# Moving the 256-column matmul streams of a fused two-block kernel out of two-bank PSUM tiles into single banks

## The chip, the cores and the metric

The kernel runs on one core of one Trainium2 chip. The metric is the device time of one execution in microseconds (us), as the median of three runs. "Faster" or "slower" below means a change of that time.

## The reference, cut to what matters

Two transformer-like blocks run one after the other on 256 tokens of width 1024, all in fp32:

```python
# block 1
proj = rms_norm(x, ln_mix_g) @ w_in
a_out = gmlp_spatial_gating(...)          # 512 channels
b_out = banded_chunk_attention(...)       # 8 heads of 64
x = x + concat([a_out, b_out]) @ w_out
x = x + peer_ffn(rms_norm(x, ln_ffn_g), w_query, sub_keys, expert_u, expert_v)
# block 2
y_pool, y_sb, y_x = (three branches) @ (w_pool_o, w_sb_o, w_x_o)
merged = gates[0] * y_pool + gates[1] * y_sb + gates[2] * y_x
h = x + rmsnorm(merged @ w_out, norm_mix_post)
gu = rmsnorm(h, norm_ffn_pre) @ w_ffn_in
out = h + rmsnorm((silu(gu[:, :2816]) * gu[:, 2816:]) @ w_ffn_out, norm_ffn_post)
```

peer_ffn picks 16 of 16384 experts per head and token; the kernel computes it densely, as two passes over all 128 x 128 experts with gates that are zero for those not picked.

## The kernel before, in words

Every large product is made of three fp32r matmuls per 128 x 128 weight block: high part of the weight times high part of the activation (line 180), the same weight times the low part of the activation (181), and the low part of the weight times the high activation (182). One *projection* is `project`: 8 weight blocks of a [128, 1024] weight tile, 24 matmuls of 256 columns (the 256 tokens), all accumulated in one 256-column stretch of PSUM, which is half a bank.

Weights stream through one pipeline that follows a fixed list. `ahead()` is called once per projection: it issues the DMA of the next raw tile (line 166), the ScalarE copy that makes its high part (`wh`, 171), runs an optional function `between`, and then issues the VectorE subtraction that makes the low part (`wl`, 116). Each engine works strictly in the order in which the program issues its instructions, so whatever stands behind one of these copies on ScalarE or VectorE waits for it.

PSUM has eight banks, given out by one pool with three tags of two buffers each: `u` and `g` are tiles of one bank (`bank()`), `y` is a tile of two banks (`pair()`). A new tile of a tag takes the buffer of the tile before the last one of the same tag, and a matmul into it waits for the last instruction that read that buffer.

The places that the change and the prediction touch, in order of the program:

- `mixer_a`, the q/k projections (loop over i = 0 to 7): their outputs alternate between `u` and `y`. Each is read twice on ScalarE, as a square (line 345) and as a scaled copy (346). For i of 2 and more these two stand behind the weight copies of `ahead()`. For i = 0 and 1 they come first, but behind what the previous step issued, among it four squares of x (line 214).
- `mixer_a`, `out(half, jp)`: eight output tiles of two projections of 12 matmuls each, e = 0 and 1. Seven write the two banks of a `y` tile, and one VectorE add (507) takes both into x. The last (half 0, jp 3) writes two `g` banks, with one add each (517), so that the first add can run beside the second projection.
- `experts`: the first two query projections run interleaved (`project2`, 198 to 201) into the two banks of a `y` tile.
- `mixer_c`, cross branch (loop over i = 0, 1): four projections of six matmuls into one `y` tile of 1024 columns, then one VectorE multiply (1055) of all 1024. Then the loop over j = 0 to 7: two projections of 12 matmuls into a `y` tile, one VectorE multiply (1067), and for j below 6 a gate projection into `u`.
- `ffn`: gate and up projections of 22 feature tiles j. Tile 0 goes to a `y` tile, tile 1 to `u`, tiles from 2 on to `g` and `u` in turn. The row norm `rs` (1181) is ready only after tile 3; the first VectorE multiply (1144) of tile 0 stands behind it.

Of the kernel before, what the change touches and what calls it, by code (L numbers as in the profile page):

```python
# [15 lines left out]
KD = 8  # L16
# [39 lines left out]
class Prog:  # L56
# [136 lines left out]
    def project2(self, pss, ws, xh, xl):  # L193

        for k in range(KD):
            for ps, w in zip(pss, ws):
                wh, wl = self.cols(w, k)
                self.mm(ps, wh, xh[:, k, :], start=(k == 0), stop=False)
                self.mm(ps, wl, xh[:, k, :], start=False, stop=False)
            for ps, w in zip(pss, ws):  # L200
                self.mm(ps, self.cols(w, k)[0], xl[:, k, :], start=False, stop=(k == KD - 1))
# [86 lines left out]
    def mixer_a(self):  # L288
# [3 lines left out]
        with tc.tile_pool(name="sa", bufs=1) as sa, tc.tile_pool(name="we", bufs=2) as we:  # L292
# [35 lines left out]
            for i in range(8):  # L328
                ps = self.pair()[:, 0, 0:S] if i % 2 else bank()
# [150 lines left out]
            def out(half, jp, gates=()):  # L480
                w = self.take()
                last = not half and jp == 3
                if last:
                    ps = [bank("g"), bank("g")]
                else:
                    pair = self.pair()[:, :, 0:S]
                    ps = [pair[:, 0, :], pair[:, 1, :]]

                def part(es, ks):
                    for e in es:  # L490
                        for k in ks:
                            wh, wl = self.cols(w, e * 4 + k)
                            self.mm3(ps[e], wh, wl, cath[:, half * 4 + k, :], catl[:, half * 4 + k, :], k == 0, k == 3)
# [6 lines left out]
                if not last:  # L500
# [5 lines left out]
                    def between():  # L506
                        tt(out=x, in0=pair, in1=x, op=ALU.add)
# [5 lines left out]
                for e in range(2):  # L513
                    j = 2 * jp + e
                    if last:
                        part((e,), range(4))
                        tt(out=self.x[:, j, :], in0=ps[e], in1=self.x[:, j, :], op=ALU.add)
# [163 lines left out]
    def experts(self):  # L681
        nc, tc, a, c = self.nc, self.tc, self.a, self.c
        with tc.tile_pool(name="sg", bufs=1) as sg:
# [32 lines left out]
            for hp in range(16):  # L716
                if hp == 0:
                    first = self.pair()
                    first = [first[:, 0, 0:S], first[:, 1, 0:S]]
# [138 lines left out]
    def mixer_c(self):  # L858
        nc, tc, a, c = self.nc, self.tc, self.a, self.c
        mm, act, tt, ts, stt = self.mm, self.act, self.tt, self.ts, self.stt  # L860
        with tc.tile_pool(name="sc", bufs=1) as sc, tc.tile_pool(name="wc", bufs=1) as wc:
# [187 lines left out]
            for i in range(2):  # L1049
                w = self.take()  # L1050
                ps = self.pair().rearrange("p e (j t) -> p (e j) t", j=2)
                for j in range(4):
                    self.project(ps[:, j, :], w, brh, brl, 8, 2, j * 2)
                g = gate[:, 16 + 4 * i:20 + 4 * i, :]
                self.ahead(between=lambda: tt(out=g, in0=ps, in1=g, op=ALU.mult))
            late = []
            for j in range(KD):
                w = self.take()
                ys = self.pair()
                for b in range(2):  # L1060
                    self.project(ys[:, b, 0:S], w, brh, brl, 4 * b, 4, 4 * b)

                def merge():
# [3 lines left out]
                    tt(out=m, in0=ys[:, :, 0:S], in1=gate[:, j:j + 9:8, :], op=ALU.mult)  # L1067
# [260 lines left out]
```

## Time and profile before

| what | value |
|---|---|
| median of 3 runs | 1305.72 us (1305.24 to 1305.84) |
| the profiled execution | 1305.5 us |
| its span, first to last instruction | 1303.7 us |
| TensorE (PE) busy | 1291.5 us, 99% |
| VectorE (DVE), ScalarE (ACT) busy | 73%, 52% |
| mean granted TensorE clock | 0.999 |

All times of the trace are counted from the start of the span. "Busy" of PE counts overlapping matmuls once; one 256-column matmul is shown as about 0.28 us long, but the next starts some 0.115 us later, so what counts is the distance between starts. "Wait" rows name the engine and line whose signal ended an idle time. The reading goes from the chain of work that ended last, to the waits of PE, to the distance between matmul starts, and then to the places where a PSUM buffer changes hands.

### The profile page before, as it was taken

The numbers are of one execution on the slowest core, as the hardware profiler recorded it, in microseconds if no ns is written. First come the engines' busy times: TensorE is split into PE (matmuls) and PEld (weight loads), VectorE is DVE, ScalarE is ACT, GpSimd is POOL, SyncE is SP. The second block draws the span as 40 slices with busy tenths as digits, with TensorE's granted clock in tenths as the row PEclk, the third lists the DMA queues.
The fourth block names the chain that finished last, engine by engine and source line by source line (L and its number), as shares of the span: only waits on it lengthen the run. The fifth ranks groups of instructions, "written<-read, shape, count | busy, mean of one in ns | idle before, by whom it ended". The sixth has DMA issues, their size and how long they took to land.

```text
span 1303.7 us, 27324 instructions
## 1 busy us (share of the span) xinstructions
PE 1291.5 (99%) x11518; PEld 1256.1 (96%) x11518; DVE 945.8 (73%) x1517; ACT 673.0 (52%) x935; POOL 1.6 (0%) x9
## 2 busy tenths in 40 slices
PE   9999999999999999999999999999999999999998
PEld 8799999999999999999999999999999999999986
DVE  5567899878888887799985665556567576776743
ACT  7575454454544444444444554444677646655542
POOL 0000000000000000000000000000000000000000
PEclk9999999999999999999999999999999999999999
DMA  8545466655655555555556755564644456455652
GB/s 273 188 128 179 162 196 197 196 191 193 190 184 176 170 173 176 182 173 170 175 165 194 257 186 193 192 194 149 228 147 147 147 193 217 160 189 193 194 186 74
DMA packets 65211, 237.14 MB, mean 182 GB/s; under 512 B 7360, under 2 KB 7488, under 8 KB 64576
## 3 DMA queue, kind: packets, MB, share of 16 engines
q1 hardware_dynamic: 64800, 233.30, 54.8%
q10 hardware_dynamic: 288, 2.10, 0.5%
q8 instruction: 90, 1.47, 0.4%
q14 instruction: 33, 0.27, 0.1%
HBM read 233.27 MB, written 2.10 MB: 181 GB/s over the span
## 4 chain that ended last, share of the span: by engine, by line
PE 94%; DVE 3%; ACT 2%; issue 1%; DMA 1%; SPq 0%; DVEq 0%; ACTq 0%
PE u L180 20%; PE u L181 19%; PE u L182 19%; PE g L180 7%; PE g L181 7%; PE g L182 7%; PE y L180 3%; PE y L182 3%; PE y L181 3%; PE y L669 2%; DVE wl L116 1%; ACT wh L171 1%; PE y L870 1%; DMA raw<-w_in_t 1%; PE y L846 1%
## 5 line engine op out<-in xcount | busy, mean ns | idle before, releaser
L116 DVE TENSOR_TENSOR wl<-raw,wh 128x1024 fp32r<-128x1024 f32 x426 | 519.1, 1222 | 271.4 <-ACT wh L171 270.7
L171 ACT ACTIVATE wh<-raw 128x1024 fp32r<-128x1024 f32 x426 | 451.1, 1060 | 485.5 <-PE u L181 376.6
L180 PE MATMUL u<-nh,wh 128*128 128x256 f32 x2176 | 609.6, 280 | 0.2 <-ACT big L1017 0.2
L181 PE MATMUL u<-nl,wh 128*128 128x256 f32 x2176 | 602.4, 277 | 0.9 <-DVE nl L733 0.5
L182 PE MATMUL u<-nh,wl 128*128 128x256 f32 x2176 | 601.7, 277 | 0.7 <-DVE wl L116 0.7
L180 PEld LDWEIGHTS u<-nh,wh 128*128 128x128 f32 x2176 | 408.7, 188 | 2.8 <-issue 1.7
L181 PEld LDWEIGHTS u<-nl,wh 128*128 128x128 f32 x2176 | 408.9, 188 | 2.0 <-DVE nl L272 0.7
L182 PEld LDWEIGHTS u<-nh,wl 128*128 128x128 f32 x2176 | 408.5, 188 | 1.0 <-DVE wl L116 0.9
L180 PE MATMUL g<-nh,wh 128*128 128x256 f32 x680 | 188.2, 277 | 0.0
L182 PE MATMUL g<-nh,wl 128*128 128x256 f32 x680 | 187.8, 276 | 0.0
L181 PE MATMUL g<-nl,wh 128*128 128x256 f32 x680 | 187.8, 276 | 0.0
L180 PEld LDWEIGHTS g<-nh,wh 128*128 128x128 f32 x680 | 127.6, 188 | 0.3 <-issue 0.3
L182 PEld LDWEIGHTS g<-nh,wl 128*128 128x128 f32 x680 | 127.7, 188 | 0.0
L181 PEld LDWEIGHTS g<-nl,wh 128*128 128x128 f32 x680 | 127.7, 188 | 0.0
L658 DVE TENSOR_TENSOR og<-ob,gT 128x1024 f16<-128x1024 f16 x64 | 41.4, 688 | 1.1
L654 DVE TENSOR_TENSOR oa<-iot,i1T 128x2048 f16<-128x2048 f16 x32 | 39.0, 1218 | 0.0
L669 PE MATMUL y<-og,oa 128*128 128x64 f16 x1024 | 35.4, 193 | 0.0
L669 PEld LDWEIGHTS <-oa 128*128 128x128 f16 x1024 | 31.6, 98 | 1.1
L1017 ACT ACTIVATE big<-u 128x256 f32<-128x256 f32 x30 | 11.5, 383 | 27.2 <-PE u L182 27.2
L181 PE MATMUL y<-brl,wh 128*128 128x256 f32 x80 | 22.4, 280 | 0.0
L180 PE MATMUL y<-brh,wh 128*128 128x256 f32 x80 | 22.3, 279 | 0.0
L182 PE MATMUL y<-brh,wl 128*128 128x256 f32 x80 | 22.3, 279 | 0.0
(342 smaller groups left out, 1388.8 us busy)
## 6 DMA issues: line engine op xcount, KB each, us to landing
raw<-peer_u SPq DMA_DIRECT2D x128, 512.0 KB, 3.6
raw<-peer_v SPq DMA_DIRECT2D x128, 512.0 KB, 3.6
raw<-w_in_t SPq DMA_DIRECT2D x50, 512.0 KB, 3.9
raw<-ffn_in SPq DMA_DIRECT2D x44, 512.0 KB, 4.0
raw<-ffn_out SPq DMA_DIRECT2D x22, 512.0 KB, 3.5
raw<-w_out SPq DMA_DIRECT2D x16, 512.0 KB, 3.6
raw<-w_query SPq DMA_DIRECT2D x16, 512.0 KB, 3.5
raw<-w_in_v SPq DMA_DIRECT2D x12, 512.0 KB, 4.4
```

The costliest lines, as they stand in the source:

```text
L116: self.tt(out=lo, in0=raw, in1=h.bitcast(F32), op=ALU.subtract)
L171: self.act(h, raw, AF.Copy)
L180: self.mm(ps, wh, xh, start=start, stop=False, **kw)
L181: self.mm(ps, wh, xl, start=False, stop=False, **kw)
L182: self.mm(ps, wl, xh, start=False, stop=stop, **kw)
L654: tt(out=split(oa), in0=row(0, P), in1=runs(i1T[:, d], P), op=ALU.is_equal)
L658: tt(out=split(og[:, s]), in0=split(ob), in1=runs(gT[:, s, d], 64), op=ALU.mult)
L669: nc.tensor.matmul(ps[:, j, :], oa[:, j, :], og[:, s, j, :], start=(s == 0), stop=(s == 1))
L846: self.mm(ps[:, j, :], w[:, k * P:(k + 1) * P], self.mem[:, k, :], start=(k == 0), stop=(k == KD - 1))
L870: mm(pss[:, t, 0:256], self.mem[:, 4 * i + k, t * P:(t + 1) * P], w[:, k * 256:(k + 1) * 256], start=(4 * i + k == 0), stop=(4 * i + k == ...
L1017: copy = lambda v, scale=1.0: lambda ps: act(v, ps, AF.Copy, scale=scale)
```

## The change

All 256-column fp32r streams that wrote a `y` tile write single banks of `u` or `g` now. The q/k projections all write `u`. In `out` the two halves of a tile share one `u` bank, the last tile too, and its second half is started with a matmul that does not clear the bank where e = 1 of jp = 0 would clear what e = 0 has summed. `project2` takes a list of outputs that share a bank with another. The first two query projections take two `g` tiles. The cross branch takes two `g` tiles per step and two VectorE multiplies of 512 columns in place of one of 1024, the branch loop takes one `g` tile per step, and tile 0 of `ffn` takes a `g` tile. The count of matmuls and their order stay; two VectorE instructions are added.

```diff
-    def project2(self, pss, ws, xh, xl):
+    def project2(self, pss, ws, xh, xl, shared=()):
+        kw = dict(skip_group_check=len(shared) > 0)
         for k in range(KD):
+            for i, (ps, w) in enumerate(zip(pss, ws)):
+                wh, wl = self.cols(w, k)
+                self.mm(ps, wh, xh[:, k, :], start=(k == 0 and i not in shared), stop=False, **kw)
+                self.mm(ps, wl, xh[:, k, :], start=False, stop=False, **kw)
             for ps, w in zip(pss, ws):
-                wh, wl = self.cols(w, k)
-                self.mm(ps, wh, xh[:, k, :], start=(k == 0), stop=False)
-                self.mm(ps, wl, xh[:, k, :], start=False, stop=False)
-            for ps, w in zip(pss, ws):
-                self.mm(ps, self.cols(w, k)[0], xl[:, k, :], start=False, stop=(k == KD - 1))
+                self.mm(ps, self.cols(w, k)[0], xl[:, k, :], start=False, stop=(k == KD - 1), **kw)
...
             for i in range(8):
-                ps = self.pair()[:, 0, 0:S] if i % 2 else bank()
+                ps = bank()
...
                 last = not half and jp == 3
-                if last:
-                    ps = [bank("g"), bank("g")]
-                else:
-                    pair = self.pair()[:, :, 0:S]
-                    ps = [pair[:, 0, :], pair[:, 1, :]]
+                ps = self.bank().rearrange("p (e t) -> p e t", e=2)
...
-                            self.mm3(ps[e], wh, wl, cath[:, half * 4 + k, :], catl[:, half * 4 + k, :], k == 0, k == 3)
+                            self.mm3(ps[:, e, :], wh, wl, cath[:, half * 4 + k, :], catl[:, half * 4 + k, :],
+                                     k == 0 and (e == 0 or jp > 0), k == 3, skip_group_check=True)
...
-                        tt(out=x, in0=pair, in1=x, op=ALU.add)
+                        tt(out=x, in0=ps, in1=x, op=ALU.add)
...
-                        tt(out=self.x[:, j, :], in0=ps[e], in1=self.x[:, j, :], op=ALU.add)
+                        tt(out=self.x[:, j, :], in0=ps[:, e, :], in1=self.x[:, j, :], op=ALU.add)
...
-                    first = self.pair()
-                    first = [first[:, 0, 0:S], first[:, 1, 0:S]]
+                    first = [self.bank("g")[:, 0:S] for _ in range(2)]
...
-                ps = self.pair().rearrange("p e (j t) -> p (e j) t", j=2)
+                ps = [self.bank("g").rearrange("p (j t) -> p j t", j=2) for _ in range(2)]
                 for j in range(4):
-                    self.project(ps[:, j, :], w, brh, brl, 8, 2, j * 2)
-                g = gate[:, 16 + 4 * i:20 + 4 * i, :]
-                self.ahead(between=lambda: tt(out=g, in0=ps, in1=g, op=ALU.mult))
+                    self.project(ps[j // 2][:, j % 2, :], w, brh, brl, 8, 2, j * 2)
+
+                def product():
+                    for j in range(2):
+                        g = gate[:, 16 + 4 * i + 2 * j:18 + 4 * i + 2 * j, :]
+                        tt(out=g, in0=ps[j], in1=g, op=ALU.mult)
+
+                self.ahead(between=product)
...
-                ys = self.pair()
+                ys = self.bank("g").rearrange("p (b t) -> p b t", b=2)
...
-            pss = [self.pair()[:, :, 0:S], self.bank().rearrange("p (e t) -> p e t", e=2)]
-            self.project2([pss[0][:, 0, :], pss[0][:, 1, :], pss[1][:, 0, :]], [self.take() for _ in range(3)], self.nh, self.nl)
+            pss = [self.bank(t).rearrange("p (e t) -> p e t", e=2) for t in "gu"]
+            self.project2([pss[0][:, 0, :], pss[0][:, 1, :], pss[1][:, 0, :]], [self.take() for _ in range(3)], self.nh, self.nl, (1,))
```

No instruction changes its place on PE, but some change what they wait for. Three places of the PE order follow (line, operation, output <- inputs, columns of the output; in brackets the engine whose signal the instruction waits for, `Activation` being ScalarE). The number behind a name tells one tile from the next of the same tag; lines of the changed kernel can be numbered one higher.

First, PE at the q/k projections of `mixer_a`: the end of the projection i = 3, the two small products of head lengths (326), the start of i = 4. Before:

```order
L182 MATMUL y_277<-nh_74,wl_180 128x256
L326 MATMUL g_147<-cst_70,qsq_224 128x2 [waits Activation_49]
L326 MATMUL g_147<-cst_70,qsq_224 128x2
L180 MATMUL u_313<-nh_74,wh_184 128x256
L181 MATMUL u_313<-nl_75,wh_184 128x256
L182 MATMUL u_313<-nh_74,wl_185 128x256 [waits DVE_49]
```

and now:

```order
L182 MATMUL u_277<-nh_74,wl_180 128x256
L327 MATMUL g_147<-cst_70,qsq_224 128x2 x2
L180 MATMUL u_313<-nh_74,wh_184 128x256 [waits Activation_49]
L181 MATMUL u_313<-nl_75,wh_184 128x256
L182 MATMUL u_313<-nh_74,wl_185 128x256 [waits DVE_49]
```

The output of i = 3 is `u` in place of `y`, and the first matmul of i = 4 waits for ScalarE: for the scaled copy that empties the `u` buffer of i = 2. The first matmul of i = 3 likewise waits for the copy of i = 1.

Second, PE in the last call of `out`: the end of half e = 0 and the start of e = 1. Before:

```order
L180 MATMUL g_1214<-cath_144,wh_1063 128x256
L181 MATMUL g_1214<-catl_145,wh_1063 128x256
L182 MATMUL g_1214<-cath_144,wl_1064 128x256
L180 MATMUL g_1215<-cath_144,wh_1063 128x256
L181 MATMUL g_1215<-catl_145,wh_1063 128x256
L182 MATMUL g_1215<-cath_144,wl_1064 128x256
```

and now:

```order
L180 MATMUL u_1214<-cath_144,wh_1063 128x256
L181 MATMUL u_1214<-catl_145,wh_1063 128x256
L182 MATMUL u_1214<-cath_144,wl_1064 128x256
L180 MATMUL u_1214<-cath_144,wh_1063 128x256 [waits DVE_49]
L181 MATMUL u_1214<-catl_145,wh_1063 128x256
```

Both halves are one tile now, and the first matmul of e = 1 waits for VectorE: for the add that reads half e = 0 of the same bank.

Third, PE in `ffn`: the end of tile 3, the spreading of the row norm, the start of tile 4. Before:

```order
L182 MATMUL u_14111<-nh_74,wl_14002 128x256
L239 MATMUL y_14136<-cst_70,rstd_14139 128x128 [waits DVE_49]
L239 MATMUL y_14136<-cst_70,rstd_14139 128x128
L180 MATMUL g_14185<-nh_74,wh_14046 128x256
L181 MATMUL g_14185<-nl_75,wh_14046 128x256
```

and now:

```order
L182 MATMUL u_14115<-nh_74,wl_14006 128x256
L240 MATMUL y_14140<-cst_70,rstd_14143 128x128 [waits DVE_49]
L240 MATMUL y_14140<-cst_70,rstd_14143 128x128
L180 MATMUL g_14189<-nh_74,wh_14050 128x256 [waits DVE_49,PE_49]
L181 MATMUL g_14189<-nl_75,wh_14050 128x256
```

Tile 4 takes the `g` buffer of tile 0 now, so its first matmul waits for the VectorE multiply that reads tile 0. In the cross branch the step i = 1 takes the two `g` buffers of step i = 0 in the same way, and its first matmul waits for the first of the two multiplies.

## Rows read from the trace of the kernel before

**Rows 1.** The page: busy times, and the chain that ended last.
```profile
PE 1291.5 (99%) x11518; PEld 1256.1 (96%) x11518; DVE 945.8 (73%) x1517; ACT 673.0 (52%) x935; POOL 1.6 (0%) x9
...
PE 94%; DVE 3%; ACT 2%; issue 1%; DMA 1%; SPq 0%; DVEq 0%; ACTq 0%
```
**Rows 2.** Waits of PE: us in total, times, longest (first and last of eleven).
```profile
PE u L255 <- POOL zeros L248: 1.0, 1, 1.0
...
PE g L397 <- ACT sp L392: 0.2, 1, 0.2
```
**Rows 3.** Instruction groups: first matmuls of each triple into y (count | busy, mean ns).
```profile
L180 PE MATMUL y<-brh,wh 128*128 128x256 f32 x80 | 22.3, 279 | 0.0
L180 PE MATMUL y<-cath,wh 128*128 128x256 f32 x56 | 16.1, 287 | 0.1
L180 PE MATMUL y<-nh,wh 128*128 128x256 f32 x32 | 9.3, 291 | 0.3 <-ACT wh L171 0.3
L198 PE MATMUL y<-nh,wh 128*128 128x256 f32 x32 | 8.3, 283 | 0.2 <-ACT nh L269 0.2
```
**Rows 4.** Windows of 24 matmuls: length, PE busy (x with edges), clock, DMA.
```profile
1048.35:1051.08 2.73, 2.73 (x26) 1.00 0.82 282
1051.08:1053.91 2.83, 2.83 (x27) 1.00 0.59 181
109.35:112.17 2.82, 2.82 (x26) 1.00 0.52 186
117.82:120.65 2.83, 2.83 (x27) 1.00 0.81 307
174.75:177.47 2.72, 2.72 (x27) 1.00 0.65 203
```
**Rows 5.** Timeline of ACT at the q/k projections: start, length.
```profile
17.70 1.06 ACT L171 ACTIVATE wh<-raw 128x1024 fp32r<-128x1024 f32 x1 [1.72 <-DMA raw<-w_in_t]
18.66 1.32 ACT L214 ACTIVATE big<-big 128x256 f32<-128x256 f32 x4
20.15 0.46 ACT L346 ACTIVATE big<-y,vecs 128x256 f32<-128x256 f32 x1
...
23.90 0.47 ACT L346 ACTIVATE big<-u,vecs 128x256 f32<-128x256 f32 x1
```
**Rows 6.** Timeline of PE: the first matmuls of projections i = 3 and 4.
```profile
18.79 0.37 PE L180 MATMUL y<-nh,wh 128*128 128x256 f32 x1
...
22.06 0.37 PE L180 MATMUL u<-nh,wh 128*128 128x256 f32 x1
```
**Rows 7.** Timeline at the first rstd of `experts`: the add, then PE.
```profile
123.19 1.15 DVE L219 TENSOR_TENSOR big<-big 128x512 f32<-128x512 f32 x2
...
124.40 0.38 PE L229 MATMUL y<-cst,big 128*128 128x1 f32 x2 [0.23 <-DVE big L219]
```
**Rows 8.** Timeline at the last `out`: DVE, and the first matmul of e = 1.
```profile
110.57 1.23 DVE L116 TENSOR_TENSOR wl<-raw,wh 128x1024 fp32r<-128x1024 f32 x1 [0.21 <-ACT wh L171]
...
112.50 0.42 DVE L517 TENSOR_TENSOR big<-g,big 128x256 f32<-128x256 f32 x1
...
110.76 0.28 PE L180 MATMUL g<-cath,wh 128*128 128x256 f32 x1
```
**Rows 9.** Timeline at the cross branch: DVE, and the first matmul of i = 1.
```profile
1042.70 1.23 DVE L116 TENSOR_TENSOR wl<-raw,wh 128x1024 fp32r<-128x1024 f32 x1 [0.94 <-ACT wh L171]
1043.84 1.22 DVE L1055 TENSOR_TENSOR big<-y,big 128x1024 f32<-128x1024 f32 x1
...
1042.70 0.28 PE L180 MATMUL y<-brh,wh 128*128 128x256 f32 x1
```
**Rows 10.** Timeline in `ffn`: tile 4 on PE, `rs` on ACT, the multiply on DVE.
```profile
1136.14 0.36 PE L180 MATMUL g<-nh,wh 128*128 128x256 f32 x1
...
1136.42 0.39 ACT L1181 ACTIVATE rs<-y 128x256 f32<-128x256 f32 x1 [2.17 <-PE y L239]
...
1136.84 0.69 DVE L1144 TENSOR_TENSOR gu<-y,rs 128x512 f32<-128x512 f32 x1 [1.33 <-ACT rs L1181]
```

More of the change, by code (lines that the diff above doesn't have):

```diff
@@ L1058, in mixer_c @@
                 w = self.take()
-                ys = self.pair()
+                ys = self.bank("g").rearrange("p (b t) -> p b t", b=2)
                 for b in range(2):
-                    self.project(ys[:, b, 0:S], w, brh, brl, 4 * b, 4, 4 * b)
+                    self.project(ys[:, b, :], w, brh, brl, 4 * b, 4, 4 * b)
                 def merge():
@@ L1066, in merge @@
                     m = sc.tile([P, 2, S], F32, tag="m", name="m", bufs=2)
-                    tt(out=m, in0=ys[:, :, 0:S], in1=gate[:, j:j + 9:8, :], op=ALU.mult)
+                    tt(out=m, in0=ys, in1=gate[:, j:j + 9:8, :], op=ALU.mult)
                     tt(out=m[:, 0, :], in0=m[:, 0, :], in1=m[:, 1, :], op=ALU.add)
```

## The prediction, made before the changed kernel was run

> **What bounds the kernel now.** I began with the page: PE is busy for 1291.5 of 1303.7 us, and 94% of the chain that ended last is PE [rows 1]. Then I read all waits of PE. There are eleven, the longest 1.0 us, the shortest 0.2 us [rows 2]; so nothing outside PE paces it for long, neither the weight copies on ACT and DVE nor the DMAs. Two things follow. Time that PE spends on a matmul is time of the kernel. And a new wait of PE of more than some tenths of a us has hardly an old wait to disappear into.
>
> The third view is the distance between matmul starts, which the busy time of one matmul doesn't show. A stretch of 24 matmuls into `u` took 2.73 us, the next 24 into `y` 2.83 us [rows 4]. That is 113.8 and 117.9 ns for one, at a granted clock of 1.00 in both. This is the only thing the change can win, so I ask what sets it, and how often it occurs.
>
> The last view is the timeline at each place where a PSUM buffer now changes hands earlier, to see when its last reader was done.
>
> **The gain: the spacing of the moved streams.** The groups into `y` with 256 columns begin with 80, 56, 32 and 32 first matmuls [rows 3], three matmuls to each: 600 in all. If every one went from the wide spacing to the narrow one, that is 600 x (117.9 - 113.8) = 2.5 us; this is the upper end. But the tag is not what decides alone. 24 matmuls into two `g` banks, each bank by itself, took 2.82 us, and 24 into `u` at the start of `experts` 2.83 us, while another 24 into `u` took 2.72 us, all at clock 1.00 [rows 4]. So the wide spacing also stands in single banks, and it seems to be a state of the stream that outlives a change of bank: the stretch into `g` follows one into `y` with the same operands, and the slow one into `u` follows the interleaved pair in `y`. In the branch loop, `y` with `brh` is wide and `u` with `nh` narrow, but there the activations change together with the bank. The change moves the bank and leaves the operands. I take a quarter of the bound, 0.6 us, since the rows nearest to the change (same operands, single bank) kept the wide spacing. The lower end is below nothing: four new breaks in the stream can leave the stretch behind them in the wide state, at 0.1 us for 24 matmuls, so -0.4 us.
>
> By the Trainium skill (TensorE: Matmul & The Clock Gate, section "Back-to-back issue gap") the spacing follows from the number of columns, about N/2.4 + 2.5 ns, which is 109 ns for 256 by its formula, with no part for the bank. The trace shows two spacings, both above that, so the formula doesn't explain them; but taken at its word that the bank has no part, the gain is nil and the sum below ends 0.6 us higher.
>
> **The cost: four new waits of PE.** The others of the new waits are met long before. For the time from a release to the waiting matmul I take 0.06 us, as between the add that ends at 123.19 + 1.15 = 124.34 and the PE instruction at 124.40 [rows 7].
>
> *q/k projections.* Outputs had four buffers (two `u`, two `y`) and have two now. Projection i = 3 starts at 18.79 [rows 6]; its buffer is now emptied by the scaled copy of i = 1. On ACT that copy stands behind a weight copy which waited 1.72 us for its DMA until 17.70, and behind four squares, and ends at 20.15 + 0.46 = 20.61 [rows 5]. None of these depends on PE at that time. So i = 3 starts at 20.67, 1.88 us late. Projection i = 4 would follow at 22.06 + 1.88 = 23.94 [rows 6], but the copy of i = 2 ends at 23.90 + 0.47 = 24.37 [rows 5], so it starts at 24.43: 2.37 us late in total. From i = 5 on the copy needed ends before the matmul that needs it. Queued behind on PE is the whole rest of the kernel. ACT and DVE have idle time here, but they give nothing back, as PE was not waiting for them.
>
> *Last output tile.* Both halves share a bank, so half e = 1 waits for the add of half e = 0. That add is not quick to come: DVE first makes a weight's low part from 110.57 and two low parts of activations, and the add runs from 112.50 to 112.92 [rows 8]. e = 1 started at 110.76, beside all this; now it starts at 112.98: 2.22 us late. A little comes back: at the first rstd PE waited 0.23 us for a DVE add [rows 7] whose inputs are delayed by less than PE. So 1.99 us.
>
> Here a rule of the Trainium skill speaks against the change (PSUM — Partial Sum Buffer, section "PSUM bank collisions raise a hardware error"): two engines must not be on one bank in the same group of 32 partitions at a time, even at different columns, so a guard has to go by bank and not by address. No run here shows a collision; the new bracket in the order at this place is such a guard. Were halves of a bank free to be used at once, this term would be nil and the sum 2.0 us lower.
>
> *Cross branch.* Step i = 0 fills both `g` buffers, and i = 1 needs the first back at once. Its first matmul started at 1042.70 [rows 9], with a second `y` tile at hand. The multiply that frees the buffer stands on DVE behind a weight's low part, which runs from 1042.70 because its high part came late; the multiply can start at 1043.84 at the earliest [rows 9]. 512 columns from PSUM take 0.69 us on DVE [rows 10], so it ends at 1044.53 and PE goes on at 1044.59: 1.89 us late. The second multiply ends some 0.7 us later, before the third projection of i = 1 asks for it (four projections of six matmuls, 0.7 us each). Two multiplies of 0.69 in place of one of 1.22 cost DVE 0.16 us twice, beside PE's work; if that cover went, 0.3 us. The branch loop asks for its buffers after the multiplies are done.
>
> *ffn.* Tile 4 takes the buffer of tile 0, which can be multiplied only when `rs` is there. ACT makes `rs` from 1136.42 to 1136.81, DVE multiplies from 1136.84 to 1137.53, while PE started tile 4 at 1136.14 [rows 10]. Now it starts at 1137.59: 1.45 us late. Tile 5 and later find their buffers free.
>
> *Free edits.* The first two query projections and the branch loop keep two buffers of one tag as before. The shared start flag changes no duration.
>
> **The sum.** 2.37 + 1.99 + 1.89 + 1.45 = 7.7 us of waits, less 0.6 us of spacing, makes +7.1 us; I take 0.1 us off for small waits in the attention part that shrink, so +7.0. On the profiled execution, 1305.5 us, this gives 1312.5 us; the median of the runs, 1305.72, is 0.2 us above that execution.
>
> **The rivals.** What a measurement of this kernel can tell from no change is about 0.2%, 2.6 us.
>
> *Spacing follows the bank.* For it: the branch loop changes between 2.73 and 2.83 us with the tag [rows 4]. Against it: the wide stretches in `g` and `u`. All waits come, and 2.5 us return: +7.7 - 2.5 - 0.1 = +5.1, 1310.6 us. Chance 0.28.
>
> *Some waits vanish in part.* If the first place is absorbed because the weights there arrive just in time (ACT waited 1.72 us for a DMA [rows 5]), 2.4 us go: +4.6, or +2.7 with the whole spacing gain, 1308.2 to 1310.1 us. Against it: PE's waits are few [rows 2]. Chance 0.11.
>
> *Not slower.* One mechanism: PE's stalls are repaid by a buffer pipeline that runs ahead meanwhile, weights being the true pace. Its place is behind the first two waits, before the expert passes; its price is their 4.4 us. It decides from the point where PE's old waits for ACT and DVE add up to more than what is added; they are eleven, the longest 1.0 us [rows 2], which speaks against. With the spacing gain in full it gives 7.7 - 4.4 - 2.5 = +0.8, 1306.3 us, and with the other two waits met early as well -2.5, 1303.0 us, within 0.2%. Chance 0.06.
>
> *Worse.* A wait delays ACT and DVE work for which PE then waits again, a further 2 us and more: above 1314.5 us. Chance 0.05.
>
> **How the numbers follow.** My forecast, waits in full and most of the spacing unmoved, has 0.50. The range reaches from the low end of the partly vanished waits, 1308.3, to the sum with no gain and four slow stretches and some knock-on: 1305.5 + 7.7 + 0.4 + 0.9 = 1314.5. Outside lie the not-slower case, the worse one and a little of the third: about 0.15. Slower by over 0.2% (above 1308.3): 0.50 + 0.28 + 0.10 + 0.05 = 0.93; within 0.2%: 0.05; faster by over 0.2%: 0.02. That the change doesn't do what it says is no case: the listed order has the new tags and waits.
>
> **What the profile would show.** PE should show waits that rows 2 doesn't have: for the scaled copy of ACT (346, now 347), the last add of `out`, line 1055 and line 1144, of about 2, 2, 1.8 and 1.3 us beyond the time of the work between. Windows of 24 matmuls with `brh` should still take 2.8 us; 2.73 makes the second case. I am wrong if these waits are there and the span grows by less than 4 us, or if PE passes the four places without a stop.

## The result, and the profile after

The changed kernel took 1316.74 us (median of 6 runs, 1313.93 to 1318.43) against 1305.78 us before (6 runs, 1305.24 to 1307.15): a ratio of 1.008 with a 95% interval of 1.0069 to 1.0092. It is 11.0 us slower; the forecast was 6.8 us slower, 1312.5 us, with a range up to 1314.5 us. The direction was right, the size was not. The spread of the executions also grew, from 1.9 to 4.5 us. The profiled execution is the fastest of the six, 1313.93 us, so 2.8 us of the median are not in this trace; the experiments look for them.

The page of the changed kernel, against [rows 1]:

```profile
PE 1292.6 (99%) x11518; PEld 1256.9 (96%) x11518; DVE 946.7 (72%) x1519; ACT 672.9 (51%) x935; POOL 1.6 (0%) x9
...
PE 93%; ACT 3%; DVE 2%; DMA 1%; issue 1%; SPq 0%; DVEq 0%; ACTq 0%
```

The span grew by 8.4 us and PE's busy time by 1.1 us only. The waits of PE, against [rows 2], where the longest was 1.0 us:

```profile
PE u L180 <- DVE big L515: 2.1, 1, 2.1
PE g L180 <- ACT wh L171: 1.8, 1, 1.8
...
PE u L180 <- ACT wh L171: 1.5, 2, 1.3
PE u L180 <- ACT big L347: 1.4, 2, 1.0
PE g L180 <- DVE gu L1146: 1.3, 1, 1.3
```

The first two rows and the last two are the four places of the forecast: the last output tile, the cross branch, the q/k projections (two waits), `ffn`. The third row lies at 7.6 and 11.9 us, at i = 0 and 1, where PE waits for its first weights; before i = 3 the lag that it left is down to 0.1 us.

For the cross branch the view names a weight copy on ACT. That is not what ended it. Both kernels have the same copies in the same order, and before, the matmul started at 1042.70 [rows 9] right behind the first copy shown here, and ahead of the next, which began at 1043.51. The same copy (second line) stands 3.6 us later in the changed kernel, with the two multiplies on DVE and the matmul behind it:

```profile
1041.61 1.06 ACT L171 ACTIVATE wh<-raw 128x1024 fp32r<-128x1024 f32 x1
...
1045.22 1.05 ACT L171 ACTIVATE wh<-raw 128x1024 fp32r<-128x1024 f32 x1
...
1047.45 1.28 DVE L1055 TENSOR_TENSOR big<-g,big 128x512 f32<-128x512 f32 x2
...
1048.29 0.41 PE L180 MATMUL g<-brh,wh 128*128 128x256 f32 x1 [1.81 <-ACT wh L171]
```

The copy ends 2 us before the matmul starts; the first multiply, of 0.69 us, ends 0.15 us before it. The wait is for the multiply, as forecast.

The last output tile, against [rows 8], as the timeline shows it on DVE and PE:

```profile
114.25 0.42 DVE L515 TENSOR_TENSOR big<-u,big 128x256 f32<-128x256 f32 x1
...
114.72 0.38 PE L180 MATMUL u<-cath,wh 128*128 128x256 f32 x1 [2.06 <-DVE big L515]
```

The add ends at 114.67, and 0.05 us later e = 1 starts. The rule of the Trainium skill that the prediction weighed (PSUM — Partial Sum Buffer, section "PSUM bank collisions raise a hardware error"), by which a program guards PSUM by bank and not by address, asks for this wait, and the trace has it.

The windows of 24 matmuls in the branch loop, against [rows 4] (u with `nh`, then g with `brh`), and then the cross branch, which comes ahead of them: its break, and the matmuls that follow it. Such a row gives the length, the busy time of PE, of the weight loads, of DVE, ACT and POOL (each with its count), the granted clock, the DMA share and GB/s:

```profile
1055.55:1058.27 2.72, 2.72 (x26) 2.72 (x25) 2.46 (x4) 1.06 (x1) 0.00 (x0) 1.00 0.65 193
1058.27:1061.10 2.83, 2.83 (x27) 2.83 (x26) 1.45 (x2) 1.33 (x2) 0.00 (x0) 1.00 0.56 164
...
1046.20:1048.28 2.08, 0.27 (x3) 0.09 (x2) 1.97 (x3) 1.97 (x3) 0.00 (x0) 1.00 0.72 252
1048.28:1051.70 3.42, 3.42 (x16) 3.42 (x17) 2.20 (x3) 0.00 (x0) 0.00 (x0) 0.52 0.60 212
```

Two things stand here. `brh` kept its wide spacing in the single bank, so the hoped-for gain is nil. And behind the break of the cross branch the granted clock is 0.52: 16 matmuls in 3.42 us, 214 ns apart in place of 118. TensorE ran at the lower of its two levels, 1.2 GHz, after a break of 2.1 us in which it had almost nothing to do. I had not reckoned with that.

PE's order is the same in both kernels, so the lag of the n-th matmul behind the n-th matmul of before can be read at each place. Four traces of the changed kernel were taken in the end; all four stand here, in us, each step by itself (small drifts between the places are left out of the rows but not of the sum). The first row is the lag at i = 4; 0.1, -0.4, 0.1 and 0.5 us of it were there before i = 3, from the start of the execution, so the waits themselves are 1.7, 1.9, 2.2 and 1.6 us:

| step | forecast | 1st trace | 2nd | 3rd | 4th |
|---|---|---|---|---|---|
| wait, q/k projections | 2.37 | 1.7 | 1.5 | 2.2 | 2.1 |
| wait, last output tile | 2.22 | 2.2 | 2.2 | 2.2 | 2.3 |
| the 28 matmuls behind it | | 0.0 | 0.1 | 0.1 | 1.6 |
| wait, cross branch | 1.89 | 2.0 | 2.0 | 2.0 | 2.0 |
| the 22 matmuls behind it | | 1.6 | 0.1 | 0.1 | 1.6 |
| from there to ffn tile 4 | | -0.3 | 1.1 | 1.1 | 0.3 |
| wait, ffn | 1.45 | 1.5 | 1.5 | 1.5 | 1.5 |
| lag at the end | 7.0 | 8.4 | 8.1 | 9.4 | 11.0 |

### The profile page after: what moved, and what is told of

Same layout as the page of the kernel before. It is cut to its first block, busy times and chain, and to the rows that moved or that the text cites. A ratio compares the mean times of both kernels' runs of the same rounds, so it can differ in the third digit from the quotient of the medians.

```text
span 1312.1 us, 27328 instructions
## 1 busy us (share of the span) xinstructions
PE 1292.6 (99%) x11518; PEld 1256.9 (96%) x11518; DVE 946.7 (72%) x1519; ACT 672.9 (51%) x935; POOL 1.6 (0%) x9
## 4 chain that ended last, share of the span: by engine, by line
PE 93%; ACT 3%; DVE 2%; DMA 1%; issue 1%; SPq 0%; DVEq 0%; ACTq 0%
PE u L180 20%; PE u L181 20%; PE u L182 19%; PE g L181 7%; PE g L180 7%; PE g L182 7%; PE y L667 2%; PE y L180 1%; PE y L182 1%; PE y L181 1%; ACT wh L171 1%; DMA raw<-w_in_t 1%; PE y L867 1%; PE y L843 1%; PE g L706 0%
## 5 line engine op out<-in xcount | busy, mean ns | idle before, releaser
L180 PE MATMUL u<-nh,wh 128*128 128x256 f32 x2208 | 619.6, 281 | 3.1 <-ACT wh L171 1.5
L182 PE MATMUL u<-nh,wl 128*128 128x256 f32 x2208 | 611.5, 277 | 1.5 <-DVE wl L116 1.5
L181 PE MATMUL u<-nl,wh 128*128 128x256 f32 x2208 | 611.7, 277 | 0.5 <-DVE nl L730 0.4
L180 PEld LDWEIGHTS u<-nh,wh 128*128 128x128 f32 x2208 | 415.0, 188 | 6.2 <-ACT wh L171 1.9
L182 PEld LDWEIGHTS u<-nh,wl 128*128 128x128 f32 x2208 | 414.8, 188 | 2.0 <-DVE wl L116 1.9
L181 PEld LDWEIGHTS u<-nl,wh 128*128 128x128 f32 x2208 | 415.2, 188 | 1.2 <-DVE nl L730 0.6
L180 PE MATMUL g<-brh,wh 128*128 128x256 f32 x80 | 23.2, 289 | 1.8 <-ACT wh L171 1.8
L181 PE MATMUL g<-brl,wh 128*128 128x256 f32 x80 | 23.2, 290 | 0.0
L182 PE MATMUL g<-brh,wl 128*128 128x256 f32 x80 | 23.0, 288 | 0.0
```

What stands on the lines that cost most here:

```text
L180: self.mm(ps, wh, xh, start=start, stop=False, **kw)
L181: self.mm(ps, wh, xl, start=False, stop=False, **kw)
L182: self.mm(ps, wl, xh, start=False, stop=stop, **kw)
```

## The experiments

Theory A: each wait costs its own length, and where the break is empty the granted clock can fall, which costs some 1.6 us more. Theory B, the rival: waits cost their length alone, and the rest is wide spacing of the matmuls over long stretches behind a break. A third question was what sets the spacing, since the change rested on that.

### One place at a time

Four kernels are the kernel before with one of the four places changed as in the change (the last of them with the new `project2` as well):

```diff
-                ps = self.pair()[:, 0, 0:S] if i % 2 else bank()
+                ps = bank()
```

> The kernel before, with only the q/k projections moved to two u buffers. Theory A (a wait costs its own length, and a break of PE of about 2 us can also drop the granted clock to half for some 3.4 us, 1.7 us more): the wait alone is 1.7 us as in the profiled execution of the changed kernel, to 2.4 us as predicted; its two breaks are 1.3 and 0.6 us, so the clock mostly stays: +1.7 to +2.4 us, 1307.4 to 1308.2 us, spread of the executions as before (2 us). Theory B (waits cost their length alone; what the timed executions are above the sum of the waits comes from the spacing of 256-column matmuls, in some executions slow over long stretches after a break): +1.7 to +2.4 us in the fastest execution and up to 4 us more in others.

```diff
-                    ps = [bank("g"), bank("g")]
+                    ps = self.bank().rearrange("p (e t) -> p e t", e=2)
+                    ps = [ps[:, 0, :], ps[:, 1, :]]
```

> The kernel before, with only the last output tile's two halves put into one u bank. The wait is 2.2 us, 0.25 us of it absorbed at the first rstd. Theory A: +2.0 us where the clock stays at 1.00 after the break, +3.7 us where it falls to half; over the executions two groups, near 1307.7 and near 1309.5 us. Theory B: +2.0 us at least, a continuous spread above it from wide spacing in the expert passes, at clock 1.00.

```diff
-                ps = self.pair().rearrange("p e (j t) -> p (e j) t", j=2)
+                ps = [self.bank("g").rearrange("p (j t) -> p j t", j=2) for _ in range(2)]
...
-                self.ahead(between=lambda: tt(out=g, in0=ps, in1=g, op=ALU.mult))
+                self.ahead(between=product)
```

> The kernel before, with only the cross branch moved to two g tiles per step. Theory A: 1.9 us of wait and in most executions 1.7 us of half clock behind it, +3.6 us, 1309.3 us, with a mean granted clock lower by 0.001. Theory B (the half clock of the one trace was chance and not due to this wait): +1.9 us, 1307.6 us, clock as before.

```diff
...
-            pss = [self.pair()[:, :, 0:S], self.bank().rearrange("p (e t) -> p e t", e=2)]
+            pss = [self.bank(t).rearrange("p (e t) -> p e t", e=2) for t in "gu"]
```

> The kernel before, with only the first tile of ffn moved from y to g. The break is 1.4 us. Theory A: +1.4 us, 1307.2 us, with a fall of the clock (+1.7 us) in few executions or none. Theory B: +1.4 us and more in some executions, from wide spacing in what follows.

All four ran beside the same runs of before (1306.51 us, 30 runs, 1305.46 to 1307.71):

| alone | median, us | executions | above before | ratio, interval |
|---|---|---|---|---|
| q/k projections | 1309.05 | 1307.8 to 1309.9 | 2.5 | 1.0020 (1.0010 to 1.0029) |
| last output tile | 1309.90 | 1308.4 to 1312.8 | 3.4 | 1.0026 (1.0017 to 1.0035) |
| cross branch | 1310.02 | 1308.0 to 1311.6 | 3.5 | 1.0027 (1.0016 to 1.0037) |
| ffn | 1308.00 | 1307.4 to 1308.6 | 1.5 | 1.0011 (1.0002 to 1.0020) |

The sum is 10.9 us, the whole of the change. So the four places explain the change, as far as intervals of some 1.2 us either way for each can show it. Two of them cost about 1.5 us more than their wait, and these two, with breaks of 2.1 and 2.3 us, have the widest spread; `ffn`, with 1.5 us, costs its wait.

The traces of these two kernels, each of the fastest execution, have clock 1.00 behind the break. But the mean granted clock of each execution is on record. Of the last output tile's executions the five fastest, 1308.4 to 1309.0 us, have 0.998 to 1.000, as the kernel before; the other six, 1309.9 to 1312.8 us, have 0.996 to 0.998. That is near the two groups of theory A, each some 1 us later than forecast.

### What is left without the four places

The changed kernel with the four places put back:

> The changed kernel with the four places put back to their old buffers: what is left are out's first seven tiles in one bank each, the two interleaved query projections in g and the branch loop in g. If the spacing went by the bank, -2.1 us, 1303.7 us. If it goes by something that stays (operands, their addresses), 0 to +0.3 us, 1305.8 to 1306.1 us; the windows of 24 matmuls with brh and cath stay at 2.82 to 2.83 us.

This was a miss: 1308.36 us against 1305.50, ratio 1.0025 (1.0015 to 1.0035). The waits of PE in it show why:

```profile
PE g L199 <- DVE big L519: 1.7, 2, 0.9
```

I had left the first two query projections in g and put the last output tile back into g, so the one waited for the other's adds. The changed kernel has no such wait, its last tile being in u. Mended, with these projections back in y:

> What the first run of the rest was meant to be: the kernel before with only out's first seven tiles in one bank each and the branch loop in g; the interleaved query projections stay in y, since in the first run their g buffers had to wait 2.6 us for the last output tile's adds. If the spacing went by the bank: -1.8 us, 1303.7 us. If not: -0.2 to +0.5 us, windows with brh and cath at 2.82 to 2.83 us.

It took 1306.44 us against 1306.29, ratio 1.0001 (0.9992 to 1.0010), which leaves room for a gain of 1.0 us at most. The windows are those of the changed kernel, g with `brh` and then u with `nh`:

```profile
1045.05:1047.88 2.83, 2.83 (x27) 2.83 (x25) 2.83 (x3) 1.06 (x1) 0.00 (x0) 1.00 0.75 219
1047.88:1050.61 2.73, 2.73 (x27) 2.73 (x26) 2.57 (x5) 1.06 (x1) 0.00 (x0) 1.00 0.77 263
```

A single bank in place of a two-bank tile is worth nothing that can be measured here.

### The changed kernel again, and with its breaks filled

> The changed kernel once more, for further executions and a second trace. Theory A: times between 1313.7 and 1319 us, in steps of about 1.7 us above 1314 by how many of the breaks the clock falls behind; a trace of a slower execution shows clock near 0.5 behind the last output tile or the ffn wait as well. Theory B: the trace of a slower execution shows clock 1.00 there and instead more stretches of 2.8 us in the expert passes.

It took 1317.31 us (4 runs, 1313.63 to 1318.46), ratio 1.0094 (1.0078 to 1.0109); again the fastest execution is the one with a trace. The same break of 2.1 us stands in it, and the clock stayed:

```profile
1046.29:1048.38 2.09, 0.28 (x4) 0.10 (x2) 1.97 (x3) 1.97 (x3) 0.00 (x0) 1.00 0.80 241
1048.38:1051.20 2.82, 2.82 (x24) 2.82 (x25) 2.27 (x3) 0.00 (x0) 0.00 (x0) 1.00 0.79 208
```

So the fall is not fixed to the place. Next, the waits of three places filled with matmuls of zeros:

```diff
+    def fill(self, n):
+        if not n:
+            return
+        ps = self.pair()[:, 0, :]
+        for i in range(n):
+            self.mm(ps[:, 0:P], self.zeros, self.zeros, start=True, stop=True)
...
+                self.fill({3: 5, 4: 2}.get(i, 0))
...
+                        self.fill(10 * e)
...
+                self.fill(8 * i)
```

> The changed kernel with the four waits filled by dummy matmuls of zeros into a free y buffer (0.22 us each pair; 1.1, 0.45, 2.2, 1.8 us; the ffn wait, 1.4 us, is left empty), so that PE waits as long as before but is busy meanwhile. Theory A: the waits stay, the clock stays at 1.00 throughout, so 1305.8 + 1.9 + 2.0 + 1.9 + 1.4 = 1313 us with a spread of no more than 2 us. Theory B: no change against the changed kernel, 1314 to 1318.5 us.

It took 1314.87 us (5 runs, 1314.27 to 1315.22), 2.4 us less than the changed kernel beside it though it does more, and the spread fell from 4.8 to 1.0 us: ratio 1.0072 (1.0058 to 1.0085). The two intervals overlap a little. Its trace has clock 1.00 at all places. It ended 1.9 us above my expectation; the fillings of the q/k projections lasted some tenths past the wait (the lag there is 2.3 us), and 1.1 us of wide spacing came between the cross branch and `ffn`, though the break of the cross branch was filled. So A holds for the larger part, and something else for a smaller one.

Filled one at a time, in the kernel before:

> The kernel before, with the last output tile's two halves in one u bank, and the wait of its second half filled with dummy matmuls (about 2.0 us). Alone, without the filling, this edit gave 1308.4 to 1312.8 us, median 3.4 us above before. Theory A (an empty break lets the clock fall in some executions): +2.0 to +2.3 us, spread at most 1.5 us. Theory B (the rest of the price is wide spacing that any break sets off, filled or not): +3.4 us and a spread of 4 us, as unfilled.

1307.80 us against 1306.29, +1.5 us (executions 1307.5 to 1309.3), ratio 1.0016 (1.0007 to 1.0025); unfilled it was +3.4.

```profile
110.50:112.70 2.20, 2.16 (x20) 1.97 (x18) 2.16 (x4) 1.19 (x5) 0.00 (x0) 1.00 0.63 182
112.70:116.00 3.30, 3.29 (x28) 3.29 (x29) 1.39 (x3) 1.61 (x5) 0.00 (x0) 1.00 0.41 154
```

The first window is the filled wait, in which PE is busy throughout; the second is what follows, at clock 1.00.

> The kernel before, with the cross branch moved to two g tiles per step and its wait filled with dummy matmuls (about 1.8 us). Unfilled this edit gave 1308.0 to 1311.6 us, median 3.5 us above before; the wait in its trace is 1.9 to 2.1 us. Theory A (what an empty break costs above its length is the fall of the clock): +1.9 to +2.2 us and a spread of at most 2 us. Theory B (wide spacing behind any break): +3.5 us as unfilled.

1308.02 us against 1305.59, +2.4 us (1306.8 to 1309.4), ratio 1.0017 (1.0008 to 1.0026); unfilled it was +3.5.

> The kernel before, with the q/k projections moved to two u buffers and the two waits filled (1.1 and 0.45 us of dummy matmuls in waits of 1.3 and 0.6 us). Unfilled: +2.5 us, 1307.8 to 1309.9 us, where the waits in its trace are 1.8 us. Theory A: +1.8 us, at most +2.3 us since the dummies can end a little after the buffer is free, spread of 1.5 us. Theory B: +2.5 us, spread as unfilled.

1307.72 us, +2.1 us (1307.0 to 1308.3), ratio 1.0016 (1.0007 to 1.0025); unfilled +2.5, with breaks of 1.6 and 0.6 us in its trace. The intervals of one place, filled and unfilled, overlap; all three medians fell, and the spreads too, from 2.2, 4.4 and 3.6 us to 1.3, 1.9 and 2.6 us in the order of the program, the last two still wider than A had them. With `ffn` as it is the sum is now 2.1 + 1.5 + 2.4 + 1.5 = 7.5 us, in place of 10.9. The forecast sum of the four waits was 7.7.

The clock on record says the same without a trace (mean over the executions of each kernel):

| place | unfilled | filled |
|---|---|---|
| q/k projections | 0.9982 | 0.9989 |
| last output tile | 0.9979 | 0.9992 |
| cross branch | 0.9983 | 0.9992 |
| ffn | 0.9992 | |
| the changed kernel (12 executions, 5 filled) | 0.9968 | 0.9990 |

The kernel before has 0.9988 to 0.9991 in four sets of 19 to 30 executions. A fall to half for 3.4 us takes 0.0013 off the mean of 1312 us. So by estimate an execution of the changed kernel has between one and two falls, and one with a single place unfilled half a fall to one; filled, none. A single execution is hard to read this way, since PE's idle time at the end of the program stands at half clock too, for some 1.5 to 5 us in the traces.

### The price of a break by itself

```diff
+    def stall(self, n):
+        ps = self.pair()[:, 0, :]
+        self.mm(ps[:, 0:P], self.zeros, self.zeros, start=True, stop=True)
+        self.tt(out=self.zero2, in0=ps[:, 0:P], in1=self.zeros, op=ALU.add)
+        for _ in range(n):
+            self.tt(out=self.zero2, in0=self.zero2, in1=self.zeros, op=ALU.add)
+        self.mm(ps[:, P:2 * P], self.zeros, self.zero2, start=True, stop=True)
...
+                if i % 8 == 4:
+                    self.stall((1, 4, 8, 12)[i // 8 % 4])
```

> The kernel before, with 16 breaks of PE of four lengths put into the first pass over the experts: PE waits for a chain of 2, 5, 9 or 13 small VectorE additions that starts from a dummy matmul (estimated 0.5 to 3 us, plus what VectorE has in hand). The breaks compute nothing. Theory A: behind the short breaks the granted clock stays 1.00, behind some of the long ones it is about 0.5 for some 3.4 us and the matmuls stand 213 ns apart, 1.7 us lost for each. Theory B: the clock stays 1.00 behind all; behind some breaks windows of 24 matmuls take 2.83 in place of 2.72 us, over many projections. Both can be seen side by side.

It took 1415.46 us, 109 us more. VectorE had weight copies in hand first, so the breaks are longer than estimated: 2.8 to 6.9 us. PE waited 70.5 us at the sixteen; some 210 matmuls at half clock, 0.1 us late each, are 21 us of the other 39, and most of the rest are the small matmuls of the breaks themselves. Here are a break of 4.5 us and two of 2.8 us, each followed by a stretch behind it:

```profile
177.54:182.00 4.46, 0.27 (x3) 0.08 (x1) 4.29 (x20) 1.51 (x2) 0.00 (x0) 0.75 0.43 141
182.00:186.20 4.20, 4.20 (x19) 4.20 (x20) 1.32 (x8) 0.00 (x0) 0.00 (x0) 0.50 0.37 125
440.64:443.46 2.82, 0.27 (x2) 0.08 (x1) 2.67 (x8) 0.49 (x2) 0.00 (x0) 1.00 0.65 206
443.46:447.00 3.54, 3.54 (x30) 3.54 (x31) 1.85 (x3) 0.30 (x1) 0.00 (x0) 1.00 0.32 122
533.95:536.80 2.85, 0.27 (x3) 0.08 (x1) 2.21 (x5) 1.52 (x2) 0.00 (x0) 1.00 0.41 161
538.20:541.20 3.00, 3.00 (x16) 3.00 (x15) 0.00 (x0) 0.00 (x0) 0.00 (x0) 0.50 0.33 126
```

Behind all twelve breaks of 3.8 us and more the matmuls stood 213 ns apart, at clock 0.50. Of the four breaks of 2.8 to 2.9 us two had no fall behind them, and two had one that began only 0.8 and 1.4 us after PE was at work again. So a break of this length loses the clock in some cases and not in others, and the slow stretch lasts 2.5 to 5.5 us. Breaks below 2.8 us, which were meant to be in this run, are not; they are in the changed kernel.

### Two more traces of the changed kernel

> The changed kernel, one more trace, to see which of its breaks have a fall of the clock behind them. Theory A: each empty break of 2 us (last output tile, cross branch) is followed by a clock near 0.5 in some executions and not in others, 1.7 us each time; 1313.5 us with none, 1317 us with two. Theory B: no trace shows it but the first.

> The same once more. Theory A: as for the run before this one, 1313.5 us without a fall, 1.7 us more for each fall that the trace shows. Theory B: no fall, times above 1314 us come from windows of 2.83 us at clock 1.00.

They took 1314.88 and 1316.55 us. The second has what A asks for, a fall behind the last output tile (second window) and one behind the cross branch (third), and one that neither theory had (first window):

```profile
9.27:12.75 3.48, 3.48 (x16) 3.48 (x17) 3.31 (x7) 3.08 (x5) 0.00 (x0) 0.52 1.03 414
...
114.90:118.44 3.54, 3.54 (x18) 3.54 (x19) 0.91 (x2) 0.86 (x2) 0.00 (x0) 0.55 0.41 140
...
1050.27:1053.64 3.37, 3.37 (x16) 3.37 (x17) 2.20 (x3) 0.00 (x0) 0.00 (x0) 0.53 0.61 188
```

The later two cost 1.6 us each, as the table above shows. The early one stands behind two breaks of 1.1 and 1.0 us with two matmuls between them, where PE waits for its first weights; the other traces have breaks like these there and no fall. At most 0.5 us of it was left at the q/k projections. In the four traces 3 of the 8 breaks of 2.1 to 2.4 us have a fall behind them, and none of the q/k and `ffn` breaks of up to 1.6 us. The other trace of this pair has no fall and is still 1.3 us slower than the second trace of the table, 0.7 us of it by the q/k waits. Here B has a point: compared with the first trace, its windows into u with `nh`, narrow there, are wide between the cross branch and `ffn`.

```profile
1055.13:1057.96 2.83, 2.83 (x27) 2.83 (x25) 2.56 (x4) 1.06 (x1) 0.00 (x0) 1.00 0.64 185
```

Ten or so such windows at 0.1 us make the 1.1 us of that row of the table. From the cross branch to `ffn` the first three traces thus lose the same beyond the wait, 1.2 to 1.3 us, with a fall or without one, and the fourth 1.9 us.

But wide stretches need no break, which B has as their cause. Here is a window of 24 matmuls in the expert passes, in the trace of the kernel before and in that of the kernel with `ffn` alone changed, whose only new wait comes 400 us later:

```profile
739.96:742.68 2.72, 2.72 (x26) 2.72 (x25) 1.82 (x4) 1.84 (x3) 0.00 (x0) 1.00 0.58 182
740.20:743.03 2.83, 2.83 (x27) 2.83 (x25) 1.83 (x4) 1.89 (x3) 0.00 (x0) 1.00 0.61 190
```

So it goes for some 250 matmuls from 727 to 757 us, 1.1 us in all, in five of the seventeen traces without the sixteen inserted breaks; the last wait of PE is over 500 us back. The matmuls with `mgh`, between the cross branch and `ffn`, are all wide in nine of the eighteen traces, among them the second kernel with the four places put back, which has no new wait, and all narrow in the others. What turns the state on and off between executions is open, and so is whether a break has a part in it.

### What sets the spacing

In the traces with the old addresses most matmuls with `cath`, `catl`, `brh` and `brl` are wide, in y, u and g alike. Those with `nh` are mostly narrow, and those with `mgh` all narrow in some traces and all wide in others. These tensors differ in their address in SBUF: the first stand at remainder 64 by 512 bytes, the others at 448. So the kernel before, with its y tiles, got other addresses:

```diff
-            self.shift(sa, 64)
+            self.shift(sa, 448)
...
-            self.shift(sa, 64)
+            self.shift(sa, 192)
...
-            self.shift(sc, 64)
+            self.shift(sc, 448)
...
+            self.shift(sc, 128)
```

> The kernel before, its PSUM tiles untouched, with the activations cath, catl, brh, brl moved by 384 bytes, so that their address in SBUF has the remainder 448 by 512 as that of nh and mgh has, in place of 64. If the spacing goes by the address of the moving operand: windows of 24 matmuls with brh fall from 2.83 to 2.72 us, 240 + 192 matmuls and more by 4.2 ns, -1.8 us, 1304.0 us. If it goes by the tag y or by the phase after a break: no change, 1305.8 us, windows of 2.83 us.

1304.43 us (11 runs, 1303.59 to 1304.61) against 1305.50 (19 runs, 1304.63 to 1306.32): ratio 0.9991 (0.9982 to 1.0000); no execution is as slow as the fastest of before. The gain is 1.1 us of the 1.8 expected. In the branch loop y with `brh` (first and third window; the second is u with `nh`) is narrow now:

```profile
1042.10:1044.82 2.72, 2.72 (x27) 2.72 (x25) 2.61 (x3) 1.97 (x3) 0.00 (x0) 1.00 0.76 209
1047.54:1050.26 2.72, 2.72 (x27) 2.72 (x25) 2.65 (x5) 1.06 (x1) 0.00 (x0) 1.00 0.75 270
1050.26:1052.98 2.72, 2.72 (x27) 2.72 (x25) 1.51 (x2) 1.33 (x2) 0.00 (x0) 1.00 0.73 191
```

All 240 matmuls with `brh` and `brl` went from wide to narrow, with the tag unchanged; in the sixteen traces with the old address at least 190 of them are wide. So for these the address counts. It is not the whole rule: `mgh`, at remainder 448 all along, is wide in this very trace, and of the matmuls with `cath` whose distance can be read 112 of 182 stayed wide, the first ten of sixteen groups of 12. I put that down to two weight buffers at remainder 384, which no view here shows, and moved these buffers too:

> The kernel with cath, catl, brh, brl at remainder 448, and in addition the two weight buffers of mixer_a that stand at remainder 384 moved by 128 bytes to remainder 0, as the other weights have. In the first address run all matmuls with those weights kept the wide spacing, those of brh with weights at 0 became narrow. If the pair of remainders decides: the 135 matmuls with these weights and the cath stretch become narrow, another -0.5 to -1 us, 1303.5 to 1304 us. If a break sets the spacing there: no change, 1304.4 us.

1304.58 us against 1306.29, ratio 0.9991 (0.9982 to 1.0000): the same gain. 70% of the matmuls with `cath` are still wide. For them the address is not the cause, or not alone. Both kernels have medians some 0.1% below the kernel before, with intervals that just reach no change.

## Why the prediction was wrong in size

**Waits: right, place by place.** All four waits stand where the forecast put them. The last output tile was forecast at 2.22 and measured at 2.2, `ffn` 1.45 and 1.5, the cross branch 1.89 and 2.0, the q/k projections 2.37 and, without the lag that was there before i = 3, 1.6 to 2.2. The last was over-sized, in the first trace because its start hung on a DMA: the weight copy that waited 1.72 us in [rows 5] waited 0.98 us in the first trace after, and the squares and the copy that frees the buffer came 0.6 us sooner. The 0.23 us that were to come back at the first rstd did not: PE waits 0.16 to 0.23 us there in all four traces. Three places filled and `ffn` as it is sum to 7.5 us against 7.7; with intervals of some 1.2 us for each, so close an agreement is partly luck.

**The step that failed is the price of a break.** "The cost: four new waits of PE" counted each by its length, and all I allowed behind one was "the wide state, at 0.1 us for 24 matmuls, so -0.4 us", with 0.9 us for knock-on at the upper end of the range. What stands behind a break of 2 us is, in some executions, 1.6 us of half clock. Wide spacing came too, up to 1.1 us and over ten windows, not one; but such stretches also come with no break near, so that part is not shown to be a price of the breaks. The two places with such breaks cost 3.4 and 3.5 us alone, not 2.0 and 1.9. I read clock 1.00 in all windows of [rows 4] and dropped the clock from the argument. But all of PE's waits before were at most 1.0 us [rows 2]: the trace of before held no break of 2 us, so that price had to be bounded, and I left it at nothing.

By the Trainium skill (TensorE: Matmul & The Clock Gate, section "What's actually happening") the throttled state of TensorE is the default and activity releases it, with two levels of 1.2 and 2.4 GHz. The traces agree: 0.50 and 1.00 granted, 213 and 113 to 118 ns for 256 columns. With the 1.6 us measured only afterwards, falls behind the two longest breaks make 1312.5 + 2 x 1.6 = 1315.7 us, a rival that the prediction did not have.

**The gain: forecast 0.6 us, measured nil.** "A quarter of the bound" was too kind, but the rows it was taken from were the right ones: same operands in a single bank, wide as before. The rival "spacing follows the bank" falls with the kernel that keeps the four old buffers, 1.0001, and with its windows: the time alone can't tell 0.6 us from nothing, but windows with `brh` of 2.83 us as before do. The formula that the prediction took "at its word" does not fit this stream: the Trainium skill (TensorE: Matmul & The Clock Gate, section "Back-to-back issue gap") gives it for a matmul by itself, and says that in a stream of weight loads and matmuls both set the spacing.

**The rivals.** "Not slower" and "some waits vanish in part" fall with the table of lags: no wait was absorbed later. "Worse" had the right side and the wrong mechanism, ACT and DVE work that PE waits for again; there is none.

What stays open: how the excess over the waits divides between falls of the clock and wide stretches in an execution without a trace. The fourth trace, with a fall behind each of the two long breaks, ended at 1316.55 us, near the median of 1316.74; the mean clock points to one to two falls.

## What to carry to other kernels

Where PE is busy 99% of the time, giving up a PSUM buffer costs the length of the wait for its last reader, and that can be read from the timeline of the kernel before to some tenths of a us. A break of PE of some 2 us can have a second price, here 1.6 us when the clock falls; a larger spread of the executions and a lower mean clock are its marks. If the break can't go, dummy matmuls in it brought most of that back here. A single trace can differ from the next by 1.1 us of wide spacing that has nothing to do with the change. Before a stream is moved to another bank for its spacing, look at whether the same operands are as slow in the bank that is meant to be better.

## What was not expected of the hardware

- Behind breaks of TensorE of 2.1 to 2.4 us the granted clock fell to half in 3 of 10 cases (the eight of the changed kernel and the two of the kernels with one place changed), behind breaks of 2.8 us in 2 of 4, and behind 3.8 us and more in 12 of 12; behind the q/k and `ffn` breaks of up to 1.6 us in no trace. In one trace it also fell behind two breaks of 1.1 and 1.0 us in the first ten us. After breaks of 2.8 us the fall came 0.8 and 1.4 us after work had begun again.
- Matmuls of 256 columns have two spacings at full clock, 113.3 and 117.8 ns, whatever bank they write. A move of the moving operand by 384 bytes in SBUF took 240 matmuls from one to the other; elsewhere whole stretches of 144 and 250 matmuls stand in one state in some executions and in the other in the rest, with no break near them.
- Work that keeps PE busy with zeros made a kernel faster: 2.4 us less in the median of the changed kernel, with a spread of 1.0 in place of 4.8 us and a mean clock of 0.9990 in place of 0.9968.
